# Gate and up of the first FFN with tokens on the partitions, half of their k-tiles through seven products for eight, the weight sums made by accumulating transfers

## The chip, the cores and the metric

The program runs on one core of one Trainium2 chip. The metric is device time in microseconds (us) of one execution; the figure shown for a kernel is the median of several runs. The engines are named as in the profile: PE (TensorE, the matrix products), PEld (its weight loads), DVE (VectorE), ACT (ScalarE), POOL (GpSimd) and SP (SyncE, which here issues transfers). Memory transfers (DMA) run on 16 engines of their own.

## What is computed

Two transformer blocks over 256 tokens of width 2048, all in float32. The change touches the feed-forward part of the first block:

```python
D_MODEL, SEQ, D_FF = 2048, 256, 5632
hn = rmsnorm(h, ffn_norm[l])
h = h + (jax.nn.silu(hn @ w_gate[l]) * (hn @ w_up[l])) @ w_down[l]
```

Both `w_gate` and `w_up` are 2048 x 5632. Around it stand the attention mixing of the first block (`block1_mix`, `block1_out`) and the second block (`block2_mix`, `block2_out`, `block2_ffn`); their arithmetic is left as it is.

## The kernel before

**Precision.** A float32 operand is held as a pair: a high part rounded to a shorter format (fp32r in the rows), and a low part, the rest. A product of two such operands is the sum of three: high with high, high with low, low with high. For weights, ACT makes the high part (`wh`, L302) and DVE the low part (`wl`, L303); the function `hl` (L313) does the same for an activation tile of 128 features x 256 tokens.

**Weights.** `weight_plan` lists all weights in the order of their use, in units of [128, up to 2048]. `load` (L274) hands out a unit and prepares the next one, which `load_unit` (L283) brings in by one transfer from SP's queue (L293) into one of three `raw` buffers and splits in halves of 1024 columns. There are four buffers each for `wh` and `wl`, so a split waits until PE is done with the half four places earlier, and a transfer until a `raw` buffer has been split.

**Products.** In most of the kernel features lie on the partitions: the stationary operand is a weight tile of 128 x 128, the moving one the activation pair. `mm_w` (L326) makes one such step with two products, 512 wide (the high weight with both halves of the pair, L334 or L332) and 256 wide (the low weight with the high half, L335 or L331). `group_w` runs a group of two column tiles over all k-tiles. In a few places tokens lie on the partitions instead: `group_a` (L352) has 128 tokens as the stationary operand and up to 512 weight columns moving, and makes three products of equal width (L366 to L368).

**FFN 1.** `block1_ffn` (L814) walks over the 44 tiles of 128 hidden features in three parts (15, 15 and 14 tiles). For a tile it runs 16 k-tiles for gate and up alternately into two banks, 32 calls of `mm_w`. The banks are evacuated by ACT and DVE (`evac`: L375, L378, L384), then come silu (L832), the product (L835) and the split of the result (L318, L319). After a part its share of the down product follows, eight groups of two output tiles, added to the residual `hs` (L843).

**Order.** Work of other kinds (norms, attention heads) is written as tasks, generators that `tick` advances by a step (`pump`) each time that products worth 2400 ns by its own count have been issued. Apart from that the order is that of the code, with some exchange of neighbours by the tile framework, which also places the waits. PSUM's eight banks are handed out in rotation by `bank` (L267).

## Time and profile before

| | |
|---|---|
| median of 3 runs | 2541.31 us (2541.17 to 2541.9) |
| span of the profiled execution, first to last instruction | 2539.5 us |
| PE busy | 2507.1 us, 99% |
| DVE busy | 1687.7 us, 66% |
| ACT busy | 1342.7 us, 53% |
| POOL busy | 127.8 us, 5% |
| bytes moved | 458.50 MB, mean 181 GB/s |

"Busy" is the time in which an engine has an instruction under way. Matrix products overlap, so a single one lasts longer than the distance between two starts, and the pace of PE is read from the starts. "Granted clock" is the share of TensorE's full clock that the chip let it have. Of a transfer, the time shown is from its issue to its landing.

### The profile page before, as it was taken

What the parts mean: (1) busy time and instruction counts of PE and PEld (TensorE: products, weight loads), DVE (VectorE), ACT (ScalarE), POOL (GpSimd) and SP (SyncE); (2) the same over time, 40 slices, a digit from 0 to 9 for tenths busy, and PEclk for the clock granted to TensorE, in tenths of its full rate; (3) what the DMA queues carried; (4) which work ended last, traced back from release to release, by engine and by line L of the source; (5) the groups of instructions that cost most, each with busy time, mean ns of one, the idle gap of its engine ahead of it and who ended that gap; (6) DMA issues with size and microseconds to landing.
All of it is one profiled execution on the core that took longest, in us unless ns stands there. A gap on an engine that the chain in (4) does not pass through costs nothing.

```text
span 2539.5 us, 36291 instructions
## 1 busy us (share of the span) xinstructions
PE 2507.1 (99%) x14372; PEld 2194.9 (86%) x14372; DVE 1687.7 (66%) x2585; ACT 1342.7 (53%) x2101; POOL 127.8 (5%) x149
## 2 busy tenths in 40 slices
PE   9999999999999999999999999999999999999997
PEld 8988888888888888888889888887888888888886
DVE  7866765876665566556666677666876567656765
ACT  6565565555444454444465555555655455545553
POOL 3000000011000000000021000003100000000002
PEclk9999999999999999999999999999999999999998
DMA  6544445555555555555555544354455555555552
GB/s 229 203 150 150 166 177 191 183 206 207 190 186 185 190 188 183 187 192 186 179 185 174 197 152 164 134 200 164 165 184 187 189 189 184 190 191 183 190 178 96
DMA packets 68938, 458.50 MB, mean 181 GB/s; under 512 B 7648, under 2 KB 10080, under 8 KB 21792
## 3 DMA queue, kind: packets, MB, share of 16 engines
q1 hardware_dynamic: 67824, 452.75, 50.3%
q10 hardware_dynamic: 944, 3.43, 0.4%
q8 instruction: 112, 1.84, 0.3%
q14 instruction: 58, 0.48, 0.1%
HBM read 454.06 MB, written 2.10 MB: 180 GB/s over the span
## 4 chain that ended last, share of the span: by engine, by line
PE 96%; DVE 2%; issue 1%; ACT 0%; DMA 0%; POOL 0%; POOLq 0%; SPq 0%; ACTq 0%; DVEq 0%
PE acc L334 54%; PE acc L335 28%; PE acc L332 4%; PE acc L331 2%; PE acc L367 2%; PE acc L366 2%; PE acc L368 2%; PE ms L488 1%; PE ms L984 1%; PE ms L517 1%; DVE hl L322 1%; DVE mres L1201 0%; DVE res L1140 0%; DVE wl L303 0%; PE ms L441 0%
## 5 line engine op out<-in xcount | busy, mean ns | idle before, releaser
L334 PE MATMUL acc<-hl,wh 128*128 128x512 f32 x5962 | 2112.0, 397 | 9.9 <-DVE hl L322 7.0
L335 PE MATMUL acc<-hl,wl 128*128 128x256 f32 x5962 | 1670.8, 281 | 0.0
L303 DVE TENSOR_TENSOR wl<-raw,wh 128x1024 fp32r<-128x1024 f32 (+4 forms) x890 | 1053.0, 1185 | 645.4 <-ACT wh L302 640.0
L334 PEld LDWEIGHTS acc<-hl,wh 128*128 128x128 f32 x5962 | 1119.5, 188 | 268.9 <-DVE hl L322 7.4
L302 ACT ACTIVATE wh<-raw 128x1024 fp32r<-128x1024 f32 (+4 forms) x890 | 909.2, 1023 | 726.4 <-PE acc L334 613.9
L335 PEld LDWEIGHTS acc<-hl,wl 128*128 128x128 f32 x5962 | 1125.7, 189 | 10.9 <-DVE wl L303 0.6
L375 ACT ACTIVATE ev<-acc 128x256 f32<-128x256 f32 x440 | 163.6, 384 | 267.3 <-PE acc L332 263.8
L378 DVE TENSOR_TENSOR tmp<-acc,ev 128x256 f32<-128x256 f32 x409 | 163.2, 423 | 94.0 <-ACT ev L375 93.8
L332 PE MATMUL acc<-hl,wh 128*128 128x512 f32 x440 | 164.9, 396 | 0.0
L408 POOL TENSOR_TENSOR ssq<-ssq,sq 128x256 f32<-128x256 f32 x92 | 85.6, 940 | 1418.2 <-ACT sq L398 948.2
L331 PE MATMUL acc<-hl,wl 128*128 128x256 f32 x440 | 125.9, 286 | 0.0
L367 PE MATMUL acc<-wl,hl 128*128 128x512 f32 (+4 forms) x264 | 90.6, 343 | 2.7 <-DVE wl L303 2.7
L366 PE MATMUL acc<-wh,hl 128*128 128x512 f32 (+4 forms) x264 | 92.7, 351 | 0.0
L331 PEld LDWEIGHTS acc<-hl,wl 128*128 128x128 f32 x440 | 82.7, 188 | 10.6 <-issue 0.3
L332 PEld LDWEIGHTS acc<-hl,wh 128*128 128x128 f32 x440 | 83.1, 189 | 9.6
L368 PE MATMUL acc<-wh,hl 128*128 128x512 f32 (+4 forms) x264 | 90.5, 343 | 0.0
L318 ACT ACTIVATE hl<-aux 128x256 fp32r<-128x256 f32 x96 | 39.1, 410 | 57.1 <-DVE aux L1167 55.1
L384 DVE TENSOR_TENSOR aux<-tmp,rB 128x256 f32<-128x256 f32 x184 | 69.2, 417 | 0.0
L367 PEld LDWEIGHTS acc<-wl,hl 128*128 128x128 f32 x264 | 49.8, 189 | 6.0 <-DVE wl L303 3.3
L319 DVE TENSOR_TENSOR hl<-aux,hl 128x256 fp32r<-128x256 f32 x96 | 40.2, 422 | 20.8 <-ACT hl L318 20.8
L368 PEld LDWEIGHTS acc<-wh,hl 128*128 128x128 f32 x264 | 49.7, 188 | 3.0
L366 PEld LDWEIGHTS acc<-wh,hl 128*128 128x128 f32 x264 | 49.7, 188 | 2.4
(235 smaller groups left out, 1047.0 us busy)
## 6 DMA issues: line engine op xcount, KB each, us to landing
raw<-in_w_dram SPq DMA_DIRECT2D x365, 1024.0 KB, 4.8
raw<-in_w_dram SPq DMA_DIRECT2D x32, 896.0 KB, 4.5
raw<-in_w_dram SPq DMA_DIRECT2D x23, 768.0 KB, 4.2
raw<-in_w_dram SPq DMA_DIRECT2D x8, 724.0 KB, 4.2
raw<-in_w_dram SPq DMA_DIRECT2D x8, 692.0 KB, 4.0
raw<-in_w_dram SPq DMA_DIRECT2D x4, 728.0 KB, 4.2
raw<-in_w_dram SPq DMA_DIRECT2D x4, 696.0 KB, 4.0
x<-in_xT_dram SPq DMA_DIRECT2D x8, 256.0 KB, 5.7
```

What stands on the lines that cost most here:

```text
L302: nc.scalar.activation(wh[:, :b - a], raw[:, a:b], AF.Copy)
L303: nc.vector.tensor_tensor(wl[:, :b - a], raw[:, a:b], wh[:, :b - a].bitcast(F32), op=ALU.subtract)
L331: nc.tensor.matmul(acc[:, S:], wl, x[:, 0, :], start=False, stop=False)
L332: nc.tensor.matmul(acc, wh, x, start=False, stop=True)
L334: nc.tensor.matmul(acc, wh, x, start=first, stop=False)
L335: nc.tensor.matmul(acc[:, S:], wl, x[:, 0, :], start=False, stop=last)
L366: nc.tensor.matmul(acc, xh, wh, start=(k == 0), stop=False)
L367: nc.tensor.matmul(acc, xh, wl, start=False, stop=False)
L368: nc.tensor.matmul(acc, xl, wh, start=False, stop=(k == n - 1))
L375: nc.scalar.activation(e, acc[:, S:], AF.Copy)
L378: nc.vector.tensor_tensor(out, acc[:, :S], e, op=ALU.add)
L408: self.nc.gpsimd.tensor_tensor(acc, acc, sq, op=ALU.add)
```

## The change

Gate and up of FFN 1 are made with **tokens on the partitions**, in groups of 512 hidden features (`group_t`), which is four of the old tiles; the parts are 16, 16 and 12 tiles. Eight banks hold a group.

**Seven products for eight.** k-tiles 0 to 7 form four pairs (a, a + 4). With the two token halves as rows, the pair as the inner dimension, and gate and up as the two columns, a pair is a product of 2 x 2 blocks, for which Strassen's method (in Winograd's form) needs seven block products in place of eight. The combinations of activations are made once, in `block1_out` (`combos`: four for each pair, split in high and low). The weights need four sums: t3 = B12 + B22, and a chain in one buffer (`sum`), which first holds B11 and becomes t1, t2 and t4 by adding B12, B22 and B21 to it; the layout in memory has the order, and the signs are taken up in the combinations of activations and in the evacuation. Each sum is made by a **transfer that POOL issues and that adds to its destination** (`accum_op=ALU.add`): t3 when its plain part has landed, and each step of a chain when the value before has been split by ACT and DVE. Two k-tile pairs share a unit of weights, so there are two chains in a group. The fourteen pieces of 1024 columns of a group come in the order of `OPS2`: B11, B11, t3, t3, t1, t1, B22, B21, t2, t2, B22, B21, t4, t4. Each is used by two steps of three products. k-tiles 8 to 15 follow as plain products, eight pieces with four steps of three each, into four banks, three of which already hold a seven-product result that belongs there.

**Evacuation.** After the seven products ACT and DVE form four common terms in SBUF (`e1`, `v`, `w5`, `c22`); after the plain k-tiles `joined` adds each bank to its term, then silu with the norm's factor, and the product `z`. A task then transposes `z` on PE, in two batches of four through bank 7, and splits it with `hl` for the down product.

**Loading, in the whole kernel.** The weights are now a stream of pieces of up to 1024 columns (`stream`). `fill` keeps 2 pieces split ahead of use (4 in FFN 1) and fetches up to five more; there are six `raw` buffers of 1024 columns in place of three of 2048, so a transfer has at most 512 KB. In FFN 1 a fifth pair of `wh` and `wl` is added.

**Around it.** `two_groups` runs the first k-tiles of two down groups before it asks for the last activations of a part. The banks get fixed names. The reserve for descriptors of POOL's transfers is set to 2048.

```diff
+PARTS_T = ((0, 16), (16, 16), (32, 12))
+PAIRS = 4
+OPS2 = (("B11", 0), ("B11", 1), ("t3", 0), ("t3", 1), ("t1", 0), ("t1", 1), ("B22", 0), ("B21", 0),
+        ("t2", 0), ("t2", 1), ("B22", 1), ("B21", 1), ("t4", 0), ("t4", 1))
...
+            op, u = p
+            if op == "B11":
+                raw = self.wx.tile([P, 1024], F32, tag="sum", name="sum", bufs=4)
+                nc.sync.dma_start(raw, w[u][:, 0:1024])
+                self.held[u] = raw
+            elif op in ("t1", "t2", "t4"):
+                raw = self.held[u]
+            else:
+                raw = self.raw(1024)
+                v, a = {"B22": (u, 1024), "B21": (u + 1, 1024), "t3": (u + 1, 0)}[op]
+                nc.sync.dma_start(raw, w[v][:, a:a + 1024])
+                if op == "t3":
+                    nc.gpsimd.dma_start(raw, w[u][:, 1024:2048], accum_op=ALU.add)
...
+    def divide(self):
+
+        nc, w = self.nc, self.t["w"]
+        p, raw = self.raws.pop(0)
+        n = p[2] - p[1] if len(p) == 3 else 1024
+        self.split.append((p, *self.halves(raw, n)))
+        if len(p) == 2:
+            u = p[1]
+            add = {"B11": (u + 1, 0), "t1": (u, 1024), "t2": (u + 1, 1024)}.get(p[0])
+            if add:
+                nc.gpsimd.dma_start(raw, w[add[0]][:, add[1]:add[1] + 1024], accum_op=ALU.add)
...
+    def two_groups(self, key, xs, n, task):
+
+        accs = [self.bank("acc") for _ in range(4)]
+        for c in range((n + 7) // 8):
+            if c == 1:
+                self.finish(task)
+            for g in range(2):
+                get = self.load(*key, g, c)
+                for k in range(8 * c, min(8 * c + 8, n)):
+                    for m in range(2):
+                        self.mm_w(accs[2 * g + m], get((k - 8 * c) * 256 + 128 * m, 128), xs[k], k == 0, k == n - 1)
+        return accs
...
+        def product(i, x, w):
+            mm(i, x[0], w[0])
+            mm(i, x[0], w[1])
+            mm(i, x[1], w[0])
...
+                q, x = {"B11": (0, cut(xs[a], t0)), "B21": (1, cut(xs[b], t0)), "B22": (2, cmb(2)),
+                        "t4": (3, cut(xs[b], t1)), "t1": (4, cmb(0)), "t2": (5, cmb(1)), "t3": (6, cmb(3))}[op]
+                product(q, x, w)
+        sb = [None] * 4
+        if PAIRS:
+            e1, v, w5, c22 = [self.fz.tile([P, 512], F32, tag="ft", name="ft", bufs=4) for _ in range(4)]
+            nc.scalar.activation(e1, banks[0], AF.Copy)
+            nc.vector.tensor_tensor(v, banks[5], e1, op=ALU.subtract)
+            nc.vector.tensor_tensor(w5, banks[4], v, op=ALU.add)
+            nc.vector.tensor_tensor(v, banks[6], v, op=ALU.subtract)
+            nc.vector.scalar_tensor_tensor(c22, banks[6], -1.0, w5, op0=ALU.mult, op1=ALU.add)
+            sb = [e1, w5, v, c22]
...
+        for k in range(2 * PAIRS, KD):
+            _, wh, wl = self.take()
+            self.fill()
+            for t, ts in enumerate((t0, t1)):
+                for n in range(2):
+                    product(std[t][n], cut(xs[k], ts), [h[:, 512 * n:512 * n + 512] for h in (wh, wl)])
...
+            for t in range(2):
+                g, u = [self.joined(*r) for r in res[2 * t:2 * t + 2]]
+                r = nh.r[:, t:t + 1]
+                zt = self.fz.tile([P, 512], F32, tag="z", name="z", bufs=2)
+                nc.scalar.activation(zt, g, AF.Silu, scale=r)
+                nc.vector.scalar_tensor_tensor(zt, u, r, zt, op0=ALU.mult, op1=ALU.mult)
+                z.append(zt)
+            yield
+            yield
+            yield
+            for h in range(2):
+                yield
+                b = self.bank("tr")
+                for i in range(2):
+                    for t in range(2):
+                        o = 256 * h + 128 * i
+                        nc.tensor.transpose(b[:, 256 * i + 128 * t:256 * i + 128 * t + 128], z[t][:, o:o + P],
+                                            self.cst("ident"))
+                for i in range(2):
+                    acts.append(self.hl(b[:, 256 * i:256 * i + 256]))
```

Where the instructions stand. **DVE, before**, over one tile of gate and up: the splits of weights (L303) have the evacuation of the tile before between them (`tmp`, `aux`, `hl`).

```order
L303 TENSOR_TENSOR wl<-raw,wh 128x1024
L378 TENSOR_TENSOR tmp<-acc,ev 128x256 x2
L384 TENSOR_TENSOR aux<-tmp,rB 128x256 x2
L303 TENSOR_TENSOR wl<-raw,wh 128x1024
L835 TENSOR_TENSOR aux<-aux 128x256
L303 TENSOR_TENSOR wl<-raw,wh 128x1024
L319 TENSOR_TENSOR hl<-aux,hl 128x256
L303 TENSOR_TENSOR wl<-raw,wh 128x1024 x2
```

**DVE, now**, at the start of the fourth group: `wl_7513` is piece 4 (t3), `wl_7546` and `wl_7557` are pieces 5 and 6 (t1 of both chains), `wl_7592` is piece 9 (t2 of the first); L490 joins a bank with its term, L1031 makes `z`.

```order
L397 TENSOR_TENSOR wl_7513<-raw_7439,wh_7512 128x1024
L490 TENSOR_TENSOR ft_7376<-q_7183,ft_7376 128x512
L490 TENSOR_TENSOR ft_7375<-q_7184,ft_7375 128x512
L1031 SCALAR_TENSOR_TENSOR z_7530<-ft_7376,small_6526,z_7530 128x512
L490 TENSOR_TENSOR ft_7377<-q_7383,ft_7377 128x512
L397 TENSOR_TENSOR wl_7546<-sum_7384,wh_7545 128x1024
L1031 SCALAR_TENSOR_TENSOR z_7535<-ft_7377,small_6526,z_7535 128x512
L397 TENSOR_TENSOR wl_7557<-sum_7402,wh_7556 128x1024
L397 TENSOR_TENSOR wl_7570<-raw_7492,wh_7569 128x1024
L397 TENSOR_TENSOR wl_7582<-raw_7510,wh_7581 128x1024
L397 TENSOR_TENSOR wl_7592<-sum_7384,wh_7591 128x1024
```

The joins and the first `z` of the group before now stand ahead of the split of piece 5, the first value of a chain in `sum_7384`.

**POOL, before**, over `block1_out`, FFN 1 and what follows: norm sums, small powers and memsets; it issues no transfer.

```order
L408 TENSOR_TENSOR ssq<-ssq,sq 128x256 x13
L977 MEMSET A_13958 128x512
L408 TENSOR_TENSOR ssq<-ssq,sq 128x256 x2
L426 TENSOR_TENSOR small<-small,mhalf 128x2
L918 MEMSET aux 64x256
```

**POOL, now**, for one steady group: two adds for t3 (L374) and three for each of the two chains (L388), in one queue.

```order
L374 DMA raw_7063<-in_w_dram 128x1024
L374 DMA raw_7082<-in_w_dram 128x1024
L388 DMA sum_7027<-in_w_dram 128x1024
L388 DMA sum_7045<-in_w_dram 128x1024
L388 DMA sum_7027<-in_w_dram 128x1024
L388 DMA sum_7045<-in_w_dram 128x1024
L388 DMA sum_7027<-in_w_dram 128x1024
L388 DMA sum_7045<-in_w_dram 128x1024
```

An add and the one two rows below it work on the same buffer; there are 88 in all, where there were none.

**PE, before**, in gate and up: pairs of products, 512 and 256 wide.

```order
L334 MATMUL acc<-hl,wh 128x512
L335 MATMUL acc<-hl,wl 128x256
L334 MATMUL acc<-hl,wh 128x512
L335 MATMUL acc<-hl,wl 128x256
L334 MATMUL acc<-hl,wh 128x512
```

**PE, now**, around the first transposes in the fourth group (L1042, of the `z` of the third group); `combo` is a combination of activations.

```order
L525 MATMUL q<-wl,combo 128x512
L525 MATMUL q<-wh,combo 128x512 x2
L1042 MATMUL tr<-cc,z 128x128 x4
L525 MATMUL q<-wl,combo 128x512
L525 MATMUL q<-wh,combo 128x512
L525 MATMUL q<-wh,hl 128x512
L525 MATMUL q<-wl,hl 128x512
L525 MATMUL q<-wh,hl 128x512 x2
```

All products are 512 wide, and the transposes stand between two products of piece 7.

## Rows read from the trace of the kernel before

**Rows 1.** The profile's page: busy time, share of the span, instructions

```profile
span 2539.5 us, 36291 instructions
...
PE 2507.1 (99%) x14372; PEld 2194.9 (86%) x14372; DVE 1687.7 (66%) x2585; ACT 1342.7 (53%) x2101; POOL 127.8 (5%) x149
```

**Rows 2.** The page's chain that ended last, by engine

```profile
PE 96%; DVE 2%; issue 1%; ACT 0%; DMA 0%; POOL 0%; POOLq 0%; SPq 0%; ACTq 0%; DVEq 0%
```

**Rows 3.** Windows of FFN 1: busy of each engine, clock, DMA share, GB/s

```profile
core 0: us, PE busy (x) PEld busy (x) DVE busy (x) ACT busy (x) POOL busy (x), PEclk, DMA share, GB/s
618.00:1290.00 672.00, 672.00 (x3820) 584.77 (x3818) 407.00 (x581) 321.78 (x456) 1.31 (x3) 1.00 0.53 187
```

**Rows 4.** ACT's instructions in gate and up: start, duration, line, operands

```profile
689.18 1.06 ACT L302 ACTIVATE wh<-raw 128x1024 fp32r<-128x1024 f32 x1 [1.75 <-PE acc L334]
691.73 0.79 ACT L375 ACTIVATE ev<-acc 128x256 f32<-128x256 f32 x2 [1.49 <-PE acc L332]
...
703.03 0.79 ACT L375 ACTIVATE ev<-acc 128x256 f32<-128x256 f32 x2 [1.49 <-PE acc L332]
...
714.33 0.79 ACT L375 ACTIVATE ev<-acc 128x256 f32<-128x256 f32 x2 [1.49 <-PE acc L332]
```

**Rows 5.** DVE's instructions in the same stretch

```profile
690.27 1.23 DVE L303 TENSOR_TENSOR wl<-raw,wh 128x1024 fp32r<-128x1024 f32 x1 [1.58 <-ACT wh L302]
...
692.89 0.75 DVE L384 TENSOR_TENSOR aux<-tmp,rB 128x256 f32<-128x256 f32 x2
693.56 1.22 DVE L303 TENSOR_TENSOR wl<-raw,wh 128x1024 fp32r<-128x1024 f32 x1
694.70 0.42 DVE L835 TENSOR_TENSOR aux<-aux 128x256 f32<-128x256 f32 x1
```

**Rows 6.** PE's products 512 wide in the second block's values

```profile
1594.00 0.39 PE L366 MATMUL acc<-wh,hl 128*128 128x512 f32 x1
...
1595.81 0.40 PE L368 MATMUL acc<-wh,hl 128*128 128x512 f32 x1
...
1596.49 1.06 PE L984 MATMUL ms<-X 128*128 128x128 f32 x8
1597.30 0.48 PE L366 MATMUL acc<-wh,hl 128*128 128x512 f32 x1
1597.62 0.39 PE L367 MATMUL acc<-wl,hl 128*128 128x512 f32 x1
...
1599.93 0.40 PE L368 MATMUL acc<-wh,hl 128*128 128x512 f32 x1
```

**Rows 7.** DMA issues: tiles, queue, count, KB each, us to landing

```profile
raw<-in_w_dram SPq DMA_DIRECT2D x365, 1024.0 KB, 4.8
...
walpha<-in_walpha_dram ACTq DMA_DIRECT2D x1, 128.0 KB, 2.6
```

**Rows 8.** A window of 0.5 us inside a load (columns as in rows 3)

```profile
691.00:691.50 0.50, 0.50 (x4) 0.43 (x4) 0.50 (x1) 0.00 (x0) 0.00 (x0) 1.00 1.00 426
```

**Rows 9.** POOL's operations by line: count, busy, mean ns, idle before

```profile
L408 POOL TENSOR_TENSOR ssq<-ssq,sq 128x256 f32<-128x256 f32 x92 | 85.6, 940 | 1418.2 <-ACT sq L398 948.2 <-issue 467.7
...
L426 POOL TENSOR_TENSOR small<-small,mhalf 128x2 f32<-128x2 f32 x17 | 14.0, 823 | 279.2 <-DVE small L431 237.0 <-ACT do L873 35.3 <-ACT aux L445 5.3
```

**Rows 10.** The window of a norm in block 2 (columns as in rows 3)

```profile
1764.00:1790.00 26.00, 18.59 (x95) 14.96 (x96) 25.29 (x41) 15.41 (x36) 17.12 (x20) 0.93 0.13 50
```

More of the change, by code (lines that the diff above doesn't have):

```diff
@@ L221, in __init__ @@
         self.ns = 0
-        self.wx, self.nhalf = None, 0
-        self.unit, self.ahead = 0, None
+        self.wx, self.nhalf, self.nbank = None, 0, 0
+        self.nraw, self.raws, self.split = 0, [], []
+        self.look, self.far, self.held = 2, 4, {}
+        self.one = None
     def add(self, gen, urgent=False):
@@ new lines, in load_unit @@
+    def load_unit(self, u, cuts=None, between=None):
+        n = UNIT_COLS[u]
+        cuts = cuts or [min(a + 1024, n) for a in range(0, n, 1024)]
+        raws = []
+        for i, (a, b) in enumerate(zip([0] + cuts, cuts)):
+            raw = self.raw(b - a)
+            self.nc.sync.dma_start(raw[:, :b - a], self.t["w"][u][:, a:b])
+            raws.append((a, b, raw))
+            if between and i == 0:
+                between()
+        return self.getter(u, [(a, b, *self.halves(raw, b - a)) for a, b, raw in raws])
@@ L795, in block1_out @@
         hs, hn, ss = [], [], None
+        xg, cs = [], []
         raw = None
```

231 lines of the change are left out of this document (166 added, 65 removed).

## The prediction

> **What bounds the kernel now.** I read the page's shares first, then the chain, then the stage that the change rewrites. TensorE (PE) is busy for 99% of the span, VectorE (DVE) for 66%, and GpSimd (POOL) has 127.8 us in all [rows 1]. The chain that ended last is PE for 96% [rows 2]. In the stretch from 618 to 1290 us, most of FFN 1, PE is busy for 672.00 of 672 us at full clock, with DVE at 407 us and the DMA engines at 0.53 [rows 3]. So here only fewer or faster PE instructions shorten anything, and the question is whether a leaner PE still finds its operands ready. The period of a tile is read on ACT, where the evacuation of each tile starts at 691.73, 703.03 and 714.33 us [rows 4]: **11.30 us** for one tile of 128 gate and 128 up features, 32 calls of mm_w, 0.353 us each. With 44 tiles the stage is 497.2 us. Span and median differ by 1.8 us (2539.5 and 2541.3); I sum differences and add them to the median.
>
> **PE work of the new stage.** A group now covers 512 features, four old tiles, 45.2 us. Its products have 128 tokens stationary and 512 weights moving. The kernel already has such products, in the values of the second block: 8 steps from 1594.00 to 1595.81 us, and 10 from 1597.62 to 1599.93 us [rows 6], so 0.226 and 0.231, I take 0.229 us. Eight plain k-tiles need 8 x 4 x 3 = 96 of them. The other eight, as four pairs, need 7 x 4 x 3 = 84 where 96 stood. 180 x 0.229 = 41.2 us. New are 8 transposes of z, 128 wide: eight such small products take 1597.30 - 1596.49 = 0.81 us, and the product after them is 0.09 us late [rows 6]; in two batches that makes 1.0 us. PE needs **42.2 us**, 3.0 less than before: 2.0 from the seventh product saved, 2.0 from the wider shape, minus 1.0.
>
> **What feeds it.** Call the 14 weight pieces of a group's seven-product half 1 to 14 in order; PE spends 6 x 0.229 = 1.37 us on each and 2.75 us on each of the 8 plain ones. A piece must be loaded, rounded on ACT, subtracted on DVE. From ACT's start to DVE's end this takes 691.50 - 689.18 = 2.3 us [rows 4, 5]; DVE gets one through every 1.14 us (693.56 to 694.70), and a 256-wide operation every 0.375 [rows 5], so I put a 512-wide one, between them, at 0.63. Per group DVE has 22 x 1.14 + 10 x 0.63 + 4 x 0.38 = 33 us, under 42; PE covers it. There are five pairs of buffers, so piece n cannot be split before PE is done with piece n-5. That leaves DVE four pieces of lead, some 11 us of plain work, which covers the seven-product half, where its own 14 x 1.14 + 5 x 0.63 + 4 x 0.38 = 20.6 us stand against 20.2 of PE.
>
> The sums have no such cover. Pieces 5, 9 and 13 (t1, t2, t4 of the first chain) are one buffer, added to three times; 6, 10 and 14 are the second chain. Each step waits for the split of the piece four places earlier, then for POOL to issue, for the add to land, and for a new split. Let A be the time from DVE's end to the landing.
>
> **The price A.** No transfer of the kernel before adds, and POOL issues none. A 1024 KB load takes 4.8 us from issue to landing [rows 7]; the engines move 426 GB/s when full [rows 8], so 2.46 us of that are bytes and 2.3 are fixed, which the 128 KB load agrees with (2.6 in all) [rows 7]. From below, 512 KB read once and issued as fast as SP does it: 2.3 + 1.23 = 3.5 us. From above, the old contents are read too (2.46), POOL takes as long as over an addition (0.94, and its smallest operations still 0.82) [rows 9], and one plain load of 512 KB is in front (1.23): 6.9 us. I take **5.2**, the middle, near the 4.8 of the row with the same bytes in both reads, with 0.4 for POOL.
>
> **The walk through a steady group**, from PE's start on piece 1. On DVE four joins and the first z of the group before stand ahead of piece 5; they end near 2.8, since one can begin before zero. Piece 5 is split at 3.95 us, then the second z, and piece 6 at 5.7. Piece 10's sum lands at 5.7 + A = 10.9 and is split at 13.2; PE arrives at 9 x 1.37 + 0.5 = 12.8. Piece 14 lands at 18.4 and is split at 20.7; PE, unstalled, arrives at 13 x 1.37 + 1.0 = 18.8. The group loses 2A - 8.5 = **1.9 us**: 44.1 instead of 45.2. In the first group of each of the three parts no joins stand on DVE, piece 6 is split at 4.0, PE has no transposes (41.2) and reaches piece 14 at 17.8: the loss is 1.2, the group 42.4. Behind a split that waits for a sum, ACT and DVE hold the next splits and the copies of the transposes, and PE's second transposes wait for those copies, as bank 7 is the only one for them. Mostly this stands early enough. In the third and the last group the second copy is behind piece 13 while the transposes stand inside piece 12: piece 13 is split at 3.95 + 2 x (5.2 + 2.3) = 18.95, copy, transposes and the rest of piece 12 add 0.4 + 0.5 + 0.9, PE is at piece 14 at 22.2, and the loss is 3.4, 1.5 more.
>
> **The sum.** 8 x 44.1 + 3 x 42.4 + 3 x 1.0 (the transposes of a part's last group fall into the down product) + 2 x 1.5 = 486.0 us, against 497.2: -11.2. The three starts of the down product need the last activations; two_groups puts 32 calls of mm_w, 32 x 0.353 = 11.3 us, ahead, while joins, z and the four pumps to the first transposes take some 10. I allow 1 us each, +3. The rest is at nothing: the combinations in block1_out lie beside PE's 11.3 us per output group; 1024 KB transfers become two of 512 KB into as many bytes of buffer, on DMA engines half idle [rows 3]. If that cover failed anywhere it would show as a PE wait outside FFN 1. Down has the same products in parts of 16, 16 and 12. -11.2 + 3 = -8.2: **2533 us**.
>
> **Rivals.**
> *The sums are hidden.* If A is 4.2 or less, the loss is nil: 8 x 42.2 + 3 x 41.2 + 6 = 467, -30, **2511 us**. For it: the plain half gives the first step 11 us of lead, and the row below is 3.5. Against it: POOL's operations with no data to speak of already cost 0.82 us [rows 9]. Chance 0.14.
> *It cancels.* With A between 5.3 and 5.8 the losses eat the 3 us, **2541 us**. Chance 0.13.
> *The adds queue on the transfer engines; slower.* One mechanism: every add reads weights and the old buffer through the same 16 engines, so it takes 2.46 us of them instead of 1.23, and the second chain's add waits for the first's and for plain loads. Per group that is 16 x 1.23 + 8 x 2.46 = 39.4 us of engines out of 44, against 0.53 now [rows 3]; the seven-product half holds four adds and some nine loads, 21 us of engines in 20. With A = 6.9 the loss is 5.3 in eight groups and 4.6 in three: -8.2 + 11 x 3.4 = +29.2, **2571 us**. It decides from A = 5.6. For it: POOL is one queue, and pieces 5 and 6 are split only 1.75 us apart. Against it: between 9 and 10 the gap grows, and the next group's first pieces are loaded early. Chance 0.39. The Trainium skill speaks for this one: "Collectives: The Full Stack", section "The bandwidth ceiling: the fold count and why AG ≠ RS ≠ AR", says that an add in the transfer path costs nothing by itself but needs two source reads, and measures about half the rate of a copy. By that rule the lower bound of A falls away and bytes alone make it 2.3 + 2.46 = 4.8, so the hidden case goes and the sum lies between 2524 and 2571; no run here shows an add yet, so I keep the bound.
> *The clock falls.* Where PE worked 18.59 of 26 us, the granted clock averaged 0.93 [rows 10]. Waits of 2 us between products are far shorter than that stretch's; I count it into the upper end.
> That the seven products aren't made can be excluded: 84 products stand in the program's order.
>
> **How the numbers follow.** Each 0.1 us of A moves the end by 2.2 us. Forecast (A of 4.2 to 5.3): 0.34, its own range 2511 to 2536. The predicted time is its 2533. The 0.2% that a measurement can tell from no change is 5 us. Faster: 0.34 + 0.14 = 0.48. Same: 0.13. Slower: 0.39. The range leaves a tenth on each side: from 2508, a little under the hidden case, to 2576, a little over A = 6.9.
>
> **What would show it.** Right: products 0.229 us apart, a group period near 44 us, PE waiting once or twice per group at pieces 13 and 14 and behind it ACT waiting for a sum; adds that land 5 us after the split. Wrong: no PE wait and periods of 42 (hidden), or periods of 46 us and more with transfer engines above 0.9 over the seven-product half (queue). PE waits on DVE with the sums long landed would refute the whole chain and make DVE the bound; a wait in other stages would refute the zero for the smaller transfers.

## The result

The changed kernel takes **2603.03 us** (median of 4 runs, 2596.26 to 2605.06) against 2541.59 before: a ratio of **1.0237** (95% interval 1.0225 to 1.025). It is slower, by 61 us. The forecast was 2533 and the range ended at 2576; the measured time lies outside it. Of the announced signs, the products 0.229 us apart and the PE waits in the seven-product half appear, and the period is the one announced for the wrong case ("46 us and more with transfer engines above 0.9").

### The profile page after: what moved, and what is told of

Same layout as the page of the kernel before. It is cut to its first block, busy times and chain, and to the rows that moved or that the text cites. A ratio compares the mean times of both kernels' runs of the same rounds, so it can differ in the third digit from the quotient of the medians.

```text
span 2600.3 us, 36273 instructions
## 1 busy us (share of the span) xinstructions
PE 2515.4 (97%) x13624; PEld 2156.6 (83%) x13624; DVE 1762.3 (68%) x2553; ACT 1381.6 (53%) x2072; POOL 205.5 (8%) x237
## 3 DMA queue, kind: packets, MB, share of 16 engines
q1 hardware_dynamic: 130608, 452.78, 51.2%
## 4 chain that ended last, share of the span: by engine, by line
PE 78%; DMA 11%; DVE 5%; issue 4%; ACT 2%; POOL 0%; POOLq 0%; ACTq 0%; SPq 0%; DVEq 0%
PE acc L434 40%; PE acc L435 20%; DMA sum<-in_w_dram 9%; PE q L525 5%; PE acc L432 3%; DVE wl L397 2%; DMA raw<-in_w_dram 2%; PE acc L480 2%; PE acc L479 2%; PE acc L481 2%; PE acc L431 2%; ACT wh L396 1%; PE ms L685 1%; DVE hl L422 1%; PE ms L1209 1%
## 5 line engine op out<-in xcount | busy, mean ns | idle before, releaser
L434 PE MATMUL acc<-hl,wh 128*128 128x512 f32 x4642 | 1644.8, 397 | 9.0 <-DVE hl L422 7.8
L397 DVE TENSOR_TENSOR wl<-raw,wh 128x1024 fp32r<-128x1024 f32 (+3 forms) x860 | 1022.2, 1195 | 516.0 <-ACT wh L396 511.7
L435 PE MATMUL acc<-hl,wl 128*128 128x256 f32 x4642 | 1299.3, 281 | 0.6 <-DVE wl L397 0.6
L396 ACT ACTIVATE wh<-raw 128x1024 fp32r<-128x1024 f32 (+3 forms) x860 | 879.1, 1029 | 630.8 <-PE acc L434 416.2
L434 PEld LDWEIGHTS acc<-hl,wh 128*128 128x128 f32 x4642 | 871.3, 188 | 209.0 <-DVE hl L422 7.1
L435 PEld LDWEIGHTS acc<-hl,wl 128*128 128x128 f32 x4642 | 875.6, 189 | 10.5 <-DVE wl L397 1.9
L525 PE MATMUL q<-wh,hl 128*128 128x512 f32 x968 | 310.2, 397 | 7.9 <-ACT wh L396 7.9
L525 PEld LDWEIGHTS q<-wh,hl 128*128 128x128 f32 x968 | 184.2, 191 | 50.4 <-ACT wh L396 10.9
L525 PE MATMUL q<-wl,hl 128*128 128x512 f32 x484 | 192.2, 397 | 6.6 <-DVE wl L397 6.6
L525 PE MATMUL q<-wh,combo 128*128 128x512 f32 x352 | 129.0, 435 | 13.7 <-ACT wh L396 13.6
L432 PE MATMUL acc<-hl,wh 128*128 128x512 f32 x352 | 131.8, 395 | 0.0
L525 PEld LDWEIGHTS q<-wl,hl 128*128 128x128 f32 x484 | 92.2, 191 | 30.2 <-DVE wl L397 10.2
L431 PE MATMUL acc<-hl,wl 128*128 128x256 f32 x352 | 100.6, 286 | 0.0
```

Of the source, the lines that this page charges most:

```text
L396: nc.scalar.activation(wh[:, :n], raw[:, :n], AF.Copy)
L397: nc.vector.tensor_tensor(wl[:, :n], raw[:, :n], wh[:, :n].bitcast(F32), op=ALU.subtract)
L431: nc.tensor.matmul(acc[:, S:], wl, x[:, 0, :], start=False, stop=False)
L432: nc.tensor.matmul(acc, wh, x, start=False, stop=True)
L434: nc.tensor.matmul(acc, wh, x, start=first, stop=False)
L435: nc.tensor.matmul(acc[:, S:], wl, x[:, 0, :], start=False, stop=last)
```

## The profile after

The page's head, chain and transfer queues answer to [rows 1, 2]; the adds' DMA issues at the end (tiles, queue, count, KB, median us to landing) to [rows 7]. q1 carries the plain loads, q0 the adds of POOL.

```profile
span 2600.3 us, 36273 instructions
PE 2515.4 (97%) x13624; PEld 2156.6 (83%) x13624; DVE 1762.3 (68%) x2553; ACT 1381.6 (53%) x2072; POOL 205.5 (8%) x237
q1 hardware_dynamic: 130608, 452.78, 51.2%
q0 software_dynamic: 12672, 46.14, 9.9%
PE 78%; DMA 11%; DVE 5%; issue 4%; ACT 2%; POOL 0%; POOLq 0%; ACTq 0%; SPq 0%; DVEq 0%
sum<-in_w_dram POOLq DMA_DIRECT2D x66, 512.0 KB, 6.6
raw<-in_w_dram POOLq DMA_DIRECT2D x22, 512.0 KB, 9.7
```

Before, transfers had no visible part in the chain; now they have 11%. An add lands 6.6 us after its issue (t1, t2, t4) or 9.7 (t3). The shares of the queues give an estimate of the engine time of one transfer: 9.9% of 2600.3 us over 88 adds is **2.93 us** of all 16 engines for 512 KB; 51.2% over 452.78 MB is **1.54 us** for 512 KB of plain load.

All of the loss is in FFN 1. DVE's last addition in `block1_out` (L806 before, L1003 after) starts at 613 us in both, its last addition to the residual in FFN 1 at 1357.7 before and 1417.8 after, and the rest takes 1182 us in both. The window of FFN 1, and three of 5 us in one steady group, answer to [rows 3]:

```profile
core 0: us, PE busy (x) PEld busy (x) DVE busy (x) ACT busy (x) POOL busy (x), PEclk, DMA share, GB/s
613.00:1418.00 805.00, 751.64 (x3490) 609.99 (x3489) 523.07 (x604) 403.80 (x504) 98.73 (x114) 0.97 0.79 225
1015.00:1020.00 5.00, 3.85 (x15) 2.27 (x13) 2.36 (x2) 2.00 (x2) 0.86 (x1) 1.00 1.02 264
1020.00:1025.00 5.00, 3.01 (x9) 1.86 (x10) 3.02 (x4) 2.66 (x4) 0.86 (x1) 0.77 1.02 245
1025.00:1030.00 5.00, 5.00 (x21) 4.04 (x20) 3.29 (x4) 3.52 (x6) 0.00 (x0) 0.88 1.03 289
```

From 1015 to 1030 us the transfer engines are full while moving 245 to 289 GB/s, where a plain load reached 426 [rows 8]. PE waits, and its clock falls: it worked 3.01 of 5 us, and the granted clock there is 0.77 on average, 0.50 from 1023 to 1025 us, which is the lower of the two levels (1.2 of 2.4 GHz).

The same group on ACT, on POOL, on DVE and at PE's first product of two groups (start, duration, line, operands, the idle time before and what ended it). The two `z` rows are the evacuation that marks a group, as the `ev` rows did in [rows 4].

```profile
1005.22 0.71 ACT L1030 ACTIVATE z<-ft,small 128x512 f32<-128x512 f32 x1
1006.72 1.06 ACT L396 ACTIVATE wh<-sum 128x1024 fp32r<-128x1024 f32 x1 [0.80 <-DMA sum<-in_w_dram]
1009.89 1.06 ACT L396 ACTIVATE wh<-sum 128x1024 fp32r<-128x1024 f32 x1 [1.36 <-DMA sum<-in_w_dram]
1016.02 1.06 ACT L396 ACTIVATE wh<-sum 128x1024 fp32r<-128x1024 f32 x1 [2.69 <-DMA sum<-in_w_dram]
1020.06 1.06 ACT L396 ACTIVATE wh<-sum 128x1024 fp32r<-128x1024 f32 x1 [2.03 <-DMA sum<-in_w_dram]
1028.76 1.06 ACT L396 ACTIVATE wh<-sum 128x1024 fp32r<-128x1024 f32 x1 [1.07 <-DMA sum<-in_w_dram]
1054.95 0.71 ACT L1030 ACTIVATE z<-ft,small 128x512 f32<-128x512 f32 x1
1010.52 0.89 POOL L388 DMA_DIRECT2D sum<-in_w_dram  x1 [10.66 <-DVE wl L397]
1012.56 0.87 POOL L388 DMA_DIRECT2D sum<-in_w_dram  x1 [1.16 <-DVE wl L397]
1018.70 0.86 POOL L388 DMA_DIRECT2D sum<-in_w_dram  x1 [5.26 <-DVE wl L397]
1022.73 0.86 POOL L388 DMA_DIRECT2D sum<-in_w_dram  x1 [3.17 <-DVE hl L419]
1010.98 1.23 DVE L397 TENSOR_TENSOR wl<-sum,wh 128x1024 fp32r<-128x1024 f32 x1 [0.16 <-ACT wh L396]
1021.15 1.22 DVE L397 TENSOR_TENSOR wl<-sum,wh 128x1024 fp32r<-128x1024 f32 x1 [1.67 <-ACT wh L396]
1030.47 1.21 DVE L397 TENSOR_TENSOR wl<-sum,wh 128x1024 fp32r<-128x1024 f32 x1
1004.37 0.39 PE L525 MATMUL q<-wh,hl 128*128 128x512 f32 x1
1054.71 0.39 PE L525 MATMUL q<-wh,hl 128*128 128x512 f32 x1
```

The period is 49.7 us (mean of eight: 50.4), forecast 44.1. The ACT rows are pieces 5, 6, 9, 10 and 14, each starting when its sum has landed. The add for piece 9 is issued at 1010.52 and lands at 1016.02, 5.5 us later; the one for piece 10, issued at 1012.56, lands at 1020.06, 7.5 us later. The DVE rows are the splits of pieces 6, 10 and 14, the second chain; the PE rows are the starts on piece 1 of this group and of the next, 50.3 us apart.

## The experiments

Times are those of whole runs, to be held against the 2603 of the changed kernel; ratios are to the kernel before; "period" is that of a group; pieces are numbered as in the prediction. The theories: (1) the adds' second read, together with the plain loads, fills the transfer engines; (2) the chain of issue, POOL's order and a fixed time costs, whatever the engines carry; (3) the order on DVE, ACT and bank 7, or the clock; later (4) each add holds back the next by some 4 us; (5) a closed loop over the groups in which t1's adds come late; (6) plain loads issued at the same time as an add of the chain make it late.

### Is it the sums at all?

`nosum` leaves out all of POOL's transfers:

```diff
-                    nc.gpsimd.dma_start(raw, w[u][:, 1024:2048], accum_op=ALU.add)
+                    pass
...
-                nc.gpsimd.dma_start(raw, w[add[0]][:, add[1]:add[1] + 1024], accum_op=ALU.add)
+                pass
```

> POOL's 88 transfers are left out, the pieces of a chain are all split from the unchanged buffer (the sums are left out). Theories 1 and 2 both: PE runs through, 42.2 us per group (180 x 0.229 + 1.0), 8 x 42.2 + 3 x 41.2 + 6 in all, 2511 us. Theory 3, the order of splits, joins and transposes on DVE, ACT and bank 7, or the clock, costs the time: periods of 46 and more remain, 2553 us or more.

Measured: **2510.2 us** (ratio 0.9877, 0.9862 to 0.9892), periods of 42.2 to 42.3. Theory 3 falls as a cause of its own: without the sums that order and the clock cost nothing. The PE part of the prediction holds (42.2 us per group to 0.1 us, 2511 to 1 us). The row of FFN 1 shows PE without a gap at full clock. Held against the row of the changed kernel (805.00 us, 751.64 of them busy), PE there waits for 53 of the 93 us, and in the other 40 it is busy longer, with nearly as many products:

```profile
613.00:1325.00 712.00, 712.00 (x3484) 595.78 (x3483) 519.82 (x601) 411.66 (x503) 26.88 (x30) 1.00 0.58 192
```

`eight` sets `PAIRS = 0`: the layout, the stream and the groups alone.

> The same layout, stream of pieces, groups of 512 and evacuation, but all sixteen k-tiles as plain products: 192 products and no sums. PE needs 192 x 0.229 + 1.0 = 45.0 us per group against 45.2 before, with 3 us for the starts of down: 2542 us, within 5 of before. If the layout or the smaller transfers cost something that was put at nothing, it shows here as more than 2550.

Measured: **2539.7 us** (0.9993, 0.9984 to 1.0002), periods of 45.0. Layout and smaller transfers cost nothing, as put. With `nosum`, which has the combinations and the seven-product evacuation too, all 93 us between 2510 and 2603 come with the adding transfers and the waits for them.

### The double read

`overwrite` keeps the 88 transfers of POOL and drops only the addition:

```diff
-                nc.gpsimd.dma_start(raw, w[add[0]][:, add[1]:add[1] + 1024], accum_op=ALU.add)
+                nc.gpsimd.dma_start(raw, w[add[0]][:, add[1]:add[1] + 1024])
```

(and the same for t3)

> POOL's 88 transfers stay where they are, with the same waits and bytes, but overwrite their destination in place of adding to it (the sums are left out). Theory 1, the second read fills the transfer engines: a group's transfers take 24 x 1.54 = 37 us of the engines in place of 48, so they are no longer full; POOL's transfers land in some 5 us, the group period falls from 50.3 to 44 or less, the time to 2535 us or less. Theory 2, the chain of POOL's issue, its order and a fixed time, whatever the engines carry: landing stays near 6.6 us and more, the period near 50, the time near 2600.

Measured: **2556.8 us** (1.0057, 1.004 to 1.0075), periods of 46 to 48. Half of the 93 us goes with the addition, half stays with transfers that stand in the chain and only overwrite. Neither theory holds alone.

A DMA issue from the page of this run, and one of POOL's rows:

```profile
sum<-in_w_dram POOLq DMA_DIRECT2D x66, 512.0 KB, 4.8
```

```profile
1032.42 0.53 POOL L388 DMA_DIRECT2D sum<-in_w_dram  x1 [8.79 <-DVE wl L397]
```

They land in 4.8 us in place of 6.6, and POOL's issue takes 0.53 us in place of 0.86.

### The price of an add by itself

`alone` appends a tail to the changed kernel in which nothing else is loaded; four buffers `qa` to `qd` take one transfer, two in a row and four in a row:

```diff
+        stage((po, 0, True))
+        stage((po, 0, False), (po, 1, False))
+        stage((po, 0, True), (po, 1, True))
+        stage(*[(po, i, True) for i in range(4)])
```

> The changed kernel with a tail after its last output: with nothing else loading, 512 KB moved by SP alone, by POOL alone, added by POOL alone, then two plain and two adding transfers of POOL in a row, then four adding ones, ACT waiting for each; the tail's own time is not part of the comparison. Theory 1, adds are slow because plain loads fill the engines beside them: a lone add lands some 1.4 us after the lone plain one (4.5 to 5 us), four in a row land 1.5 to 2.9 us apart. Theory 4, adds are served one after the other, about 4 us each whatever else is loaded: two in a row land 3.5 to 4 us apart, four in some 16 us, plain ones under 2 us apart.

It was run once, and only its rows are used. The rows are ACT's reads, each waiting for a landing: the lone add; the first of two plain; two adds; the first and last of four. A window inside the four follows (columns as before).

```profile
2601.04 0.20 ACT L1502 ACTIVATE small<-qa 128x1 f32<-128x1 f32 x1 [5.54 <-DMA qa<-in_w_dram]
...
2605.92 0.20 ACT L1502 ACTIVATE small<-qa 128x1 f32<-128x1 f32 x1 [4.17 <-DMA qa<-in_w_dram]
...
2614.43 0.20 ACT L1502 ACTIVATE small<-qa 128x1 f32<-128x1 f32 x1 [5.78 <-DMA qa<-in_w_dram]
2617.21 0.20 ACT L1502 ACTIVATE small<-qb 128x1 f32<-128x1 f32 x1 [2.58 <-DMA qb<-in_w_dram]
...
2623.92 0.20 ACT L1502 ACTIVATE small<-qa 128x1 f32<-128x1 f32 x1 [5.99 <-DMA qa<-in_w_dram]
...
2632.38 0.20 ACT L1502 ACTIVATE small<-qd 128x1 f32<-128x1 f32 x1 [2.26 <-DMA qd<-in_w_dram]
```

```profile
2625.00:2630.00 5.00, 0.00 (x0) 0.00 (x0) 0.00 (x0) 0.29 (x2) 0.00 (x0) 0.50 1.00 191
```

A lone add lands 5.5 us after its buffer is free, the first of two plain transfers 1.4 us sooner (4.17); adds in a row follow 2.8 us apart ((2632.38 - 2623.92) / 3), and they alone fill the transfer engines (1.00) at 191 GB/s. That is theory 1's price, not theory 4's 4 us. So the forecast's A = 5.2 was nearly right for an add that has the engines to itself. DVE's work beside it is not what makes an add late: DVE has nothing to do in this tail, and the shortest landing in the changed kernel, 5.4 us after POOL's issue, is no longer than that of the lone add (issued at 2595.58, read at 2601.04). The Trainium skill ("Collectives: The Full Stack", section "The bandwidth ceiling: the fold count and why AG ≠ RS ≠ AR") has an add in the transfer path read two sources, at about half the rate; the trace agrees, with 2.93 us of engines against 1.54, and 191 GB/s against 426 [rows 8].

### Which adds cost?

Three runs leave out two of the eight adds of a group each, the same engine time: `not1` those of t1, `not2` those of t2, `not3` those of t3.

```diff
-            add = {"B11": (u + 1, 0), "t1": (u, 1024), "t2": (u + 1, 1024)}.get(p[0])
+            add = {"t1": (u, 1024), "t2": (u + 1, 1024)}.get(p[0])
```

(`not1`; in `not2` the entry "t1" is missing, in `not3` the add in `fetch`)

> The changed kernel without the two adds of t1 per group (t1 is then B11; the output is another). Theory 5: the loop is cut at its first step, t2's and t4's steps remain with some 3.7 us of loss by the prices of the tail (a lone add 5.5 us, one behind another 2.8 later): period 46 to 48, the time 2555 to 2577 us. If the total of engine time alone sets the loss: the same as without t3's adds, 44 or less, under 2533 us.

> The changed kernel without the two adds of t2 per group (t2 is then t1; the output is another). Theory 5: the chain has two steps in place of three; t4's adds are issued right behind the splits of pieces 9 and 10, which the buffers allow early, and the loss falls to 0 to 2 us, clearly less than without t1's or t3's adds: period 42.5 to 44.5, 2515 to 2537 us. If the total of engine time alone sets the loss: the same as in the two other runs.

> The changed kernel without the two adds of t3 per group (t3 is then B12 alone; the output is another), six adds left. Theory 5, the sums make a closed loop from group to group (t1's adds, their split, t2's, t4's, the products, and the next group's first pieces), in which t1's adds come late because t3's two stand before them on POOL and on the transfer engines: t1's land 5.5 and 8.3 us after their issue in place of 9.8 and 10.6, the lead of a group's start is back, period 46 to 48, the time 2555 to 2577 us. If the total of engine time alone sets the loss: 48 - 5.9 = 42 us per group are left, period 44 or less, under 2533 us.

Measured: `not1` 2604.9 us (1.0248, 1.0233 to 1.0263), no gain; `not2` 2581.9 (1.0152, 1.0135 to 1.0169), 21 us; `not3` 2591.3 (1.0197, 1.0181 to 1.0212), 12 us. All three expectations missed. POOL's order of the adds that are left is unchanged in all three. The total of engine time falls, since equal amounts gain 0 to 21 us; so does theory 5, since cutting the loop at t1 gains nothing. The trace of `not1` shows the rest. ACT's splits of pieces 9, 10, 13 and 14, then POOL's adds for t2 and t4 of the second chain:

```profile
1017.34 1.06 ACT L396 ACTIVATE wh<-sum 128x1024 fp32r<-128x1024 f32 x1 [4.26 <-DMA sum<-in_w_dram]
1021.31 1.06 ACT L396 ACTIVATE wh<-sum 128x1024 fp32r<-128x1024 f32 x1 [1.96 <-DMA sum<-in_w_dram]
1026.84 1.06 ACT L396 ACTIVATE wh<-sum 128x1024 fp32r<-128x1024 f32 x1 [2.46 <-DMA sum<-in_w_dram]
1032.55 1.06 ACT L396 ACTIVATE wh<-sum 128x1024 fp32r<-128x1024 f32 x1 [3.44 <-DMA sum<-in_w_dram]
1013.54 0.86 POOL L388 DMA_DIRECT2D sum<-in_w_dram  x1 [0.92 <-DVE wl L397]
1023.98 0.86 POOL L388 DMA_DIRECT2D sum<-in_w_dram  x1 [3.10 <-DVE hl L419]
1014.35 1.47 SPq L360 DMA_DIRECT2D raw<-in_w_dram  x2
1020.82 4.63 SPq L360 DMA_DIRECT2D raw<-in_w_dram  x2
```

The second chain's adds land 7.8 us (1013.54 to 1021.31) and 8.6 us (1023.98 to 1032.55) after their issue, and beside each of them SP issues two plain loads (last two rows): the splits of the plain pieces that stand next to those of the sums on DVE free the buffers into which SP loads further pieces. That is theory 6.

In `not2` the wait moves from t2 to t4. Both chains' adds for t4 are now issued 1.1 us apart (1005.66 and 1006.80 us), with four plain loads from SP between 1002.96 and 1009.40, and the second lands 9.5 us after its issue:

```profile
1006.80 0.86 POOL L388 DMA_DIRECT2D sum<-in_w_dram  x1 [0.27 <-issue]
1016.34 1.06 ACT L396 ACTIVATE wh<-sum 128x1024 fp32r<-128x1024 f32 x1 [3.62 <-DMA sum<-in_w_dram]
```

The steps of the prediction's walk can be read in every run. In the table, times start at PE's first product on piece 1; a landing goes from DVE's end on a split of the second chain to ACT's start on the next; the loss by the walk is DVE's end on piece 14 less 18.8, where PE would arrive; the measured one is the distance of two such starts of PE less 42.2. All are means, in us, of the five groups that have a group of their part before and behind them.

| run | piece 6 split | landings for t2, t4 | loss by the walk | loss measured |
|---|---|---|---|---|
| forecast | 5.7 | 5.2, 5.2 | 1.9 | |
| changed kernel | 7.7 | 7.4, 7.1 | 8.2 | 8.2 |
| `not1` | 6.8 | 8.4, 8.0 | 9.2 | 10.0 |
| `not2` | 7.3 | 2.0, 10.2 | 5.6 | 6.9 |
| `not3` | 5.3 | 8.3, 7.7 | 7.3 | 7.9 |
| `overwrite` | 5.4 | 6.8, 6.1 | 4.2 | 5.1 |
| `tied` | 8.6 | 7.4, 7.5 | 9.4 | 10.3 |
| `tiedless` | 5.6 | 6.6, 5.9 | 4.2 | 4.6 |
| `t3late` | 11.8 | 7.3, 7.0 | 12.0 | 11.9 |

(The last three runs follow below; in `not2` the 2.0 has no add in it.) Without t3's adds the group's start is on time, so it is they that make t1's late; part of that gain goes again to later landings of t2 and t4. Why those grow in `not1` and `not3` is not shown.

### Do the plain loads make the adds late?

`moreload` goes one way: each plain piece is loaded a second time, for nobody.

```diff
+            if PLAN[u][0][0] == "guk":
+                extra = self.wx.tile([P, 1024], F32, tag="extra", name="extra", bufs=1)
+                nc.sync.dma_start(extra, w[u][:, a:b])
```

> Beside each of the eight plain pieces of a group its 512 KB are loaded once more by SP into a buffer that nobody reads. Theory 1: the engines carry 48 + 8 x 1.54 = 60 us per group and set the period, 58 to 61 us in place of 50.3, the time 2690 us or more. Theory 4: the adds take as long as before, the period rises by 2 us at most, the time is under 2625 us.

Measured: **2684.6 us** (1.0567, 1.055 to 1.0585); the adds of the chain land in 8.7 us in place of 6.6, and the periods lie between 49 and 63. The direction is that of theory 1, the size a little less. It is no clean measure: `extra` is a single buffer, and SP, which issues the loads in order, waits 398 us in all for it. This run, `lessload`, `tied` and `tiedless` also have three `sum` buffers in place of four.

The other way is to leave plain loads out. `lessload` splits one buffer, loaded once, for all plain pieces. `thinload` keeps their buffers but loads 64 of their 1024 columns.

> All adds stay, but the eight plain pieces of a group are not loaded (one buffer, loaded once, is split for all of them; the output is another). Theory 1: the engines carry 8 x 1.54 + 8 x 2.93 = 35.8 us in place of 48 per group, the adds land in 4.5 to 5.2 us in place of 6.6, the period falls to 44 or less, the time to 2535 us or less. Theory 2: the period stays near 50, the time near 2600.

> As the changed kernel, with POOL's order as there, but of each of the eight plain pieces of a group only 64 of 1024 columns are loaded, and one buffer, loaded once, is split in place of all of them (the output is another). The engines carry 8 x 2.9 + 8 x 1.5 = 35 us per group in place of 48. Theory 1 with the price of the tail (a lone add 5.5 us, one behind another 2.8 later): piece 10 is split at 14.7, piece 14 at 22.5, where PE would be at 18.8, so a period near 46, the time near 2555 us. If the plain loads beside the adds are no part of it: period near 50, near 2600 us.

Measured: 2645.1 and 2638.6 us (1.0397, 1.0378 to 1.0417; 1.0387, 1.037 to 1.0405), slower with fewer bytes, against every theory. Here the order in which the framework had placed the transfers on POOL had moved. POOL's rows of `lessload` in one group, and ACT's split of piece 9:

```profile
961.29 0.86 POOL L394 DMA_DIRECT2D sum<-in_w_dram  x1 [24.09 <-DVE wl L403]
963.96 0.86 POOL L394 DMA_DIRECT2D sum<-in_w_dram  x1 [1.81 <-DVE wl L403]
972.11 0.86 POOL L380 DMA_DIRECT2D raw<-in_w_dram  x1 [7.29 <-DVE ft L496]
974.73 0.88 POOL L380 DMA_DIRECT2D raw<-in_w_dram  x1 [1.75 <-DVE wl L403]
975.29 2.12 POOL L394 DMA_DIRECT2D sum<-in_w_dram  x2
986.17 1.06 ACT L402 ACTIVATE wh<-sum 128x1024 fp32r<-128x1024 f32 x1 [11.41 <-DMA sum<-in_w_dram]
```

The two `raw` adds are t3 of the next group. With buffers free earlier they are placed ahead of t2's adds, and these then stand behind them on POOL and on the engines; ACT waits 11.4 us. In `thinload` some stand among t4's adds. Both runs show how dear a foreign add inside the chain is, and decide nothing on the loads. So the order was held. In `tied`, ACT copies one column of the last sum of a group into t3's buffer before that is loaded:

```diff
+                if op == "t3" and self.last is not None:
+                    nc.scalar.activation(raw[:, 0:1], self.last[:, 0:1], AF.Copy)
```

`tiedless` adds the edit of `lessload` to it.

> Control for the next run: as the changed kernel, but the next group's loads of t3 are held until the last add of this group's chain has landed (ACT copies one column from that buffer first). In the changed kernel they come later than that anyway. Every theory: within 10 us of 2603.

> The same, with POOL's order so held, and the eight plain pieces of a group not loaded (one buffer, loaded once, is split for all of them; the output is another). Theory 6, adds are late because plain loads issued at the same time share the transfer engines with them (the second chain's t2 and t4 land 8 to 9 us after DVE's end): they fall to the prices of the tail (a lone add 5.5 us, one behind another 2.8 later), piece 14 is split at 22.5 where PE would be at 18.8, period near 46, the time 2545 to 2565 us. If the pairs of adds alone do it: within 10 us of the control.

Measured: `tied` 2611.7 us (1.028, 1.0263 to 1.0297), `tiedless` **2567.7** (1.0108, 1.0093 to 1.0123), 44 us less; its period is 47.5 in the mean. The chain's adds land at the price of the tail, 5.6 us after their issue where `tied` has 6.7:

```profile
sum<-in_w_dram POOLq DMA_DIRECT2D x66, 512.0 KB, 5.6
```

Theory 6 holds: of the 101 us by which `tied` lies above `nosum`, 44 go with the plain loads. They had delayed the group's start (piece 6 at 8.6 us, now 5.6) as well as the landings in the chain (14.9 us in all, now 12.5). What is left of the loss, 57.5 us above `nosum`, is the chain of adds itself: by the walk two landings of 12.5 us in all cost 4 us per group even with few loads beside them. `tiedless` against `lessload`, the same bytes with and without the order held, is worth 77 us. The upper end of what was expected, 2565, was missed by 3 us.

### Order and clock

`t3late` moves t3 from places 3 and 4 to 11 and 12 in the order of pieces, B22 and B21 to 3 and 4.

```diff
-OPS2 = (("B11", 0), ("B11", 1), ("t3", 0), ("t3", 1), ("t1", 0), ("t1", 1), ("B22", 0), ("B21", 0),
-        ("t2", 0), ("t2", 1), ("B22", 1), ("B21", 1), ("t4", 0), ("t4", 1))
+OPS2 = (("B11", 0), ("B11", 1), ("B22", 0), ("B21", 0), ("t1", 0), ("t1", 1), ("B22", 1), ("B21", 1),
+        ("t2", 0), ("t2", 1), ("t3", 0), ("t3", 1), ("t4", 0), ("t4", 1))
```

> The order of the fourteen pieces alone is changed: t3 goes from places 3 and 4 to places 11 and 12, B22 and B21 take its place. POOL's adds for t1 no longer stand behind those for t3 at a group's start, but t3's now stand between those for t2 and t4. Theory 1 (engines full, same bytes): period 50, time within 10 us of 2603. Theory 2 (only the lost lead of the first step costs): 2 to 4 us less per group, 2560 to 2580 us. Theory 4 (each add holds back the next for about 4 us): t4's adds come up to 8 us later, periods of 53 to 58, 2635 us or more.

Measured: **2642.0 us** (1.0402, 1.0386 to 1.0417), periods of 52 to 57. In POOL's rows t3's adds (1019.25 and 1020.84 us in one group) stand beside those of t1 (1019.88 and 1021.38), not between t2's and t4's as was expected: piece 6 is split 11.8 us after the group's start, the landings behind it are as before (table above). An add in front of one of the chain costs, as in `lessload`. Theory 4 named this time, but not its reason: `alone` shows 2.8 us between adds and not 4.

`warm` puts 32 small products with zeros per group where PE was thought to wait:

```diff
+                if op in ("t2", "t4") and i == 0:
+                    for _ in range(8):
+                        nc.tensor.matmul(banks[2][:, :P], self.zeros, self.zeros, start=False, stop=False)
```

> The changed kernel with eight 128-wide products with zeros ahead of pieces 9, 10, 13 and 14 of a group, 4 x 0.8 = 3.2 us of PE in places where it waits; they add nothing to the result. If the fall of the granted clock after the waits takes a part of its own of the 8 us that a group loses (at most 0.03 x 805 / 11 = 2.2 us by the granted clock of 0.97): it stays near 1.0 and the time falls by 10 to 24 us, to 2580 to 2593. If the sums alone set the period: within 5 us of 2603, and above it where the products find no wait to lie in.

Measured: **2633.9 us** (1.037, 1.0354 to 1.0385), 31 us more, nearly the whole 11 x 3.2 = 35. They found few waits to lie in: in this run PE waits most before the second transposes (44.7 us over FFN 1, for copies behind a split that waits for a sum). So it says nothing on the clock. The granted 0.97 bounds what its fall cost at 0.03 x 805 = 24 us, some 2 us per group. In the five groups of the table less is left for it: the walk, which has no clock in it, gives the whole loss of the changed kernel (8.2 of 8.2). In the group shown the slow products (1023 to 1027 us) lie in front of a wait for the sum of piece 14, from which PE starts again at 1031.74; the wait takes up what they lose.

### Sums without adding transfers

`sumdve` loads each block once and lets DVE sum in the buffers, in an order in which t3 comes at places 7 and 8. `sumboth` is the same with t3's sums on POOL. `mixed` has t1, t2 and t4 on DVE and t3 by POOL's adding transfers, early and outside any chain; `mixed2` has t3 at places 11 and 12.

```diff
+            h = self.held[p[1]]
+            eng = lambda op: nc.vector
+            if p[0] == "B11":
+                eng("t1").tensor_tensor(h["sum"], h["sum"], h["B12"], op=ALU.add)
+            elif p[0] == "B22":
+                eng("t3").tensor_tensor(h["B12"], h["B12"], h["B22"], op=ALU.add)
+            elif p[0] == "t1":
+                eng("t2").tensor_tensor(h["sum"], h["sum"], h["B22"], op=ALU.add)
+            elif p[0] == "B21":
+                eng("t4").tensor_tensor(h["sum"], h["sum"], h["B21"], op=ALU.add)
```

> Each block of weights is loaded once by SP, and DVE makes the four sums of a chain in the buffers (t1, t3, t2, t4, in another order of pieces); POOL issues nothing. DVE has 33 + 8 x 1.14 = 42.2 us per group, as much as PE. If the sums by transfer were the whole trouble: periods of 42.3 to 43.5, 2511 to 2525 us, faster than both kernels. If DVE, now as full as PE, becomes the bound in the seven-product half: periods of 44 to 46, 2530 to 2553 us.

> The sums of the chain (t1, t2, t4) on DVE as in the run with all sums there, t3 by POOL's adding transfers, issued five pieces ahead of their use and not part of a chain. DVE 33 + 6 x 1.14 = 39.8 us per group, transfer engines 18 x 1.5 + 2 x 2.9 = 33 us of 42. If only adds inside the chain hurt: periods of 42.3 to 42.8, 2511 to 2518 us. If any add holds back the loads of its time: periods of 43.5 and more, over 2523 us.

> As the run with t3 by adding transfers and the chain on DVE, with t3 at places 11 and 12 in place of 7 and 8, and t4's sums right behind the splits of t2. PE needs 42.2 us per group and ran at 43.0 there, where ACT waited 18 us in all for late transfers in front of a split. If those waits cost the rest: 2511 to 2516 us. If DVE's order does, or the starts of down: 2516 to 2521 us.

> As the run with all sums on DVE, but t3 is summed by POOL (two operations of 1024 columns per group, needed only at places 7 and 8). DVE has 39.8 us per group. If POOL works beside DVE without touching it: 2511 to 2518 us. If the two engines hold each other up on their operands in SBUF, DVE's operations beside it last longer and the time stays at 2521 us or more.

Measured: `sumdve` 2523.1 us (0.9928, 0.9914 to 0.9943); `mixed` **2518.5** (0.991, 0.9895 to 0.9925); `mixed2` 2520.0 (0.9915, 0.99 to 0.9929); `sumboth` 2541.6 (1.0001, 0.9992 to 1.001). Three beat both kernels, by 18 to 23 us against the one before. `mixed` keeps 22 adds where they have time, with periods of 42.6 to 43.9 against 42.3 without any sum (DVE's six sums in a group included): adds outside the chain are nearly free here. What its last 8 us are is open: in `mixed2`, made to remove ACT's waits for late transfers, these fall only from 18.1 to 15.8 us over FFN 1. `sumboth` shows why POOL is no help. POOL's two sums and DVE's operations beside them:

```profile
920.13 2.41 POOL L392 TENSOR_TENSOR b<-b,raw 128x1024 f32<-128x1024 f32 x1 [34.75 <-DVE sum L390]
925.01 3.27 POOL L392 TENSOR_TENSOR b<-b,raw 128x1024 f32<-128x1024 f32 x1 [2.48 <-issue]
920.32 3.31 DVE L405 TENSOR_TENSOR wl<-sum,wh 128x1024 fp32r<-128x1024 f32 x1 [0.32 <-ACT wh L404]
926.53 2.84 DVE L405 TENSOR_TENSOR wl<-raw,wh 128x1024 fp32r<-128x1024 f32 x1
```

DVE's operation takes 3.31 or 2.84 us in place of 1.22: what POOL takes over, DVE loses in waiting. The Trainium skill ("SBUF — State Buffer", section "SBUF: two separate sides") states that these two engines share a pair of ports, and that one of them holds it for a whole instruction when VectorE has two inputs in SBUF and GpSimd reads SBUF; these rows agree, each of DVE's two ends 1.1 us after POOL's.

## Why the prediction was wrong

- **What bounds, and PE's work: right.** 42.2 us were forecast for a group without waits, `nosum` has 42.2 to 42.3. For all sixteen k-tiles as plain products the same way of counting gives 192 x 0.229 + 1.0 = 45.0, and `eight` has 45.0. "Hidden" was 2511, `nosum` has 2510. The zero for layout, smaller transfers and combinations holds.
- **DVE: right. The cover of the first step: wrong.** DVE leaves PE no gap in `nosum`. But t3's and t1's adds come later than the plain half covers: ACT waits 0.80 and 1.36 us for t1 in the group shown, and piece 6 is split 7.7 us after the group's start where the walk has 5.7 (5.3 in `not3`). That is 2.0 us of loss per group that the text put at nothing.
- **The walk: right in form.** With the measured steps in place of its own it gives the loss (table above). In the group shown PE starts on piece 1 at 1004.37, DVE ends piece 6 at 1012.21, 7.84 us after it; the second chain's landings take 7.85 us (to 1020.06) and 6.39 (1022.37 to 1028.76), and DVE ends piece 14 at 1031.68, 27.3 us after the start. Less 18.8 this is 8.5; PE's next start is 50.3 us after this one, a loss of 8.1.
- **The price A: the step that failed.** 5.2 was taken for every add, and it is close for an add alone (5.5). But the term that counts twice is the add of the *second* chain, issued 2 us behind the first's, which by itself takes 2.8 us of the engines, and together with plain loads that splits next to it set free. It lands 7.8 and 6.4 us after DVE's end in this group, 8.1 and 8.9 in the one shown of `not1`: beyond even the upper bound of 6.9 in three of four. On average the two landings take 14.5 us where 10.4 were put: 4.1 us per group, twice what the late start adds.
- **The upper bound: too low.** It took transfers at the bytes they move at 426 GB/s, 1.23 and 2.46 us, 39.4 us for a group. In engine time they are 1.54 and 2.93, 16 x 1.54 + 8 x 2.93 = 48 us, nearly the period of 50.4. And it put one plain load in front of an add where two are issued beside it.
- **The rival "the adds queue on the transfer engines": this is what happened**, in its place (the seven-product half) and by its mechanism, at 2603 in place of 2571. It had a chance of 0.39, more than the forecast's 0.34. The predicted time was nevertheless the forecast's and not that of the case with the highest chance; the middle of two bounds was preferred. The reason set against the rival, that the next group's first pieces are loaded early, did not hold: their adds, for t3, and those for t1 behind them came late.
- **The clock: under-weighted as to its fall, not as to its price.** "Far shorter than that stretch's" was the argument; the clock still fell to 0.50 in places. In the steady groups its price is within what the walk leaves, next to nothing.

What is shown: without the addition the kernel gains 46 us (`overwrite`), without the plain loads 44 (`tiedless` against `tied`), without any of POOL's transfers 93. What is not settled is what the clock costs outside the groups of the table, and why the landings of t2 and t4 grow when t1's or t3's adds are left out.

## What to carry to other kernels

A transfer that adds is no free arithmetic: price it in engine time (read the queue's share), and as a step of latency wherever a consumer's split releases it. Put it where it has a long lead and no chain, as `mixed` does, and sum on an engine with room inside a chain. When splits next to the one that releases a critical transfer free buffers for prefetch, count the prefetch as sharing the engines with it.

## What the runs showed of the hardware

- 512 KB added to SBUF take 2.8 to 2.9 us of the 16 transfer engines and fill them at 191 GB/s; plain, 1.54 us.
- POOL is busy 0.86 us for the issue of an add and 0.53 us for the same transfer without it.
- Fewer bytes made the kernel slower by 36 to 42 us while transfers were placed earlier in POOL's order, and 44 us faster than its control with the order held.
- A sum of 1024 columns on POOL takes 2.4 to 3.3 us and holds up DVE's operations beside it by 1.6 to 2.1 us.
